# A decoder layer on one core: where the sums of its modulation are kept, who forms the first of them, and in what pieces the first columns of the input projection are worked off

## The chip, the core and the metric

The kernel runs on one NeuronCore of a Trainium2 chip. TensorE (PE) multiplies matrices, VectorE (DVE), ScalarE (ACT) and GpSimd (Pool) work element by element, and SyncE (SP) issues the DMA transfers. Each engine works off its own queue in order; semaphores let one engine wait for another. SBUF is the working memory on the chip, PSUM the memory of eight banks of 128 x 512 floats that TensorE writes its products to. The metric is the time of one execution on the device in microseconds (us), the median of several runs.

## The reference, cut to what matters

One layer for 512 positions and a model width of 2048. A conditioning vector gives a shift, a scale and a gate; the input is normalised, scaled and shifted, and multiplied with one wide matrix whose columns feed two branches.

```python
cond = jax.nn.silu(c)
mod = cond @ w_ada[l] + b_ada[l]                  # 2048 x 6144
shift, scale, gate = jnp.split(mod, 3, axis=-1)
h = rms_norm(x, norm_g[l]) * (1.0 + scale[:, None, :]) + shift[:, None, :]
z = h @ w_in[l]                                   # 2048 x 7184
...
y = jnp.concatenate([y_a, y_b], axis=-1) @ w_out[l]
x = x + gate[:, None, :] * y
```

Everything is in float32. Shift and scale alone need two thirds of `w_ada`, 33.6 MB, before the last part of `h` is known.

## The kernel before, in words

**Products in three.** A float32 product is made of three passes of a faster type: each operand is split into a high and a low half, and TensorE adds high x high, high x low and low x high into one PSUM bank (`mm_cols`, L143 to L145). ACT makes the high half of a weight tile (`whi`, L127), and DVE or Pool subtracts to get the low half (`wlo`, L128). The halves of `h` are `hh` and `hl`.

**The start.** `x` is loaded in four row tiles, each is squared and summed on ACT (`junk`, L311), scaled on DVE (L313) and transposed on TensorE; ACT copies the transposed blocks out as `xT` (L325). Rows of 128 columns of the model width are the 16 k-blocks. For each k-block the shift and the scale are needed, and these are sums over the 2048 rows of `w_ada`. They are not formed on TensorE: a vector engine multiplies each block of 128 rows (`ada`, loaded by `load`, L104) with a number per partition (`sc`) and adds it to an accumulator, sixteen times per group of k-blocks, and a short matmul with a column of ones (`mod`, L267, one pass per k-block and half) then adds over the partitions. `ADA` lists the nine groups: k-blocks 0 and 1 alone, then seven groups of two. `make_h` turns a group's totals into `sh` and `gs` (L272 to L274, DVE), makes `hh` on ACT (L278), a second scaled copy of `xT` on ACT (L286) and `hl` on Pool (L289).

**Where the sums lie, before.** For groups 0 and 1 there are two accumulators of 256 columns in SBUF (`acca`, L237 and L239), used in turns, all on DVE. For groups 2 to 8 the accumulator `acc` lies in PSUM, in the one bank of the tag "c" (L251, L253), and only the last of the sixteen steps writes to SBUF (`accs`). The totals `mod` use the same bank, so a group's sums begin when the totals of the group ahead have been read.

**The first columns.** While `w_ada` streams in, 14 column blocks of 128 (`s`, in two sets of seven) are worked off k-block by k-block, in chunks `CH`: within a chunk first one set over the chunk's k-blocks, then the other. Seven banks hold one set, so at a change of set it is put aside in SBUF (`sp`): ACT copies it the first time (L407), DVE adds it after that (L410). Weights come in tiles of one k-block in the first chunk and of two after that, 512 or 384 columns wide (`raw_st`, then `whi_st` and `wlo_st`, with two buffers each). Pool makes their low halves, but for the two tiles of k-block 0 that come with Pool left out (`q or kk`, L389). Steps of the sums of the next chunk's groups are spread between the weight tiles. After this stage come the attention branch, the gating branch and the output projection, nearly all TensorE; none of that is touched.

**The order.** The scheduler orders each engine's queue ahead of time, from the order of the program and priorities (`high_priority`, `issue_after`). All loads go through SP in one queue. TensorE's queue holds each `mod` at a fixed place between the products.

Of the kernel before, what the change touches and what calls it, by code (L numbers as in the profile page):

```python
# [27 lines left out]
def trunk_kernel(  # L28
# [17 lines left out]
    nc = tc.nc  # L46
# [21 lines left out]

# [1 line left out]
    ident = const.tile([P, P], F32, name="ident")  # L70
# [21 lines left out]

# [1 line left out]
    queue = []  # L94
# [72 lines left out]

# [6 lines left out]
    nc.sync.dma_start(rows[16:32, :], norm_g[0].rearrange("(a b) -> a b", b=P))
    nc.sync.dma_start(rows[32:64, :], b_ada[0, 0 : 2 * D].rearrange("(a b) -> a b", b=P))
    nc.sync.dma_start(rows[64:72, :], ln_g[0].rearrange("(a b) -> a b", b=P))
    nc.sync.dma_start(rows[72:80, :], ln_b[0].rearrange("(a b) -> a b", b=P))

    xt = []
# [23 lines left out]
    WARM = 4
    wbank = bank("c", "warm")

    def warm(src, n):
        for i in range(n):
            nc.tensor.matmul(wbank[:, 0:128], ident, src, start=True, stop=True)

    ADA = [(0, 1), (1, 1), (2, 2), (4, 2), (6, 2), (8, 2), (10, 2), (12, 2), (14, 2)]  # L210
    LANE = "DEDE"

    def ada_step(q, i):
        k0, nk = ADA[q]
        w = nk * P
        per = 4 // nk
        ga = st.tile([P, per, 2, w], F32, name=f"ada{q}_{i}", tag="ada", bufs=8)
        for s in range(2):
            load(
                ga[:, :, s, :], ada_r[:, i * per : (i + 1) * per, s, k0 * P : k0 * P + w]  # L220
            )
        if q == 0:
            warm(ga[:, 0, 1, :], WARM)
        if q in SPL:
            if i == 0:
                three = st.tile([P, 2, 256], F32, name=f"acca{q}", tag="acc", bufs=2)
                accs[q] = {
                    "D": three[:, 0, :].rearrange("p (s n) -> p s n", s=2),
                    "E": three[:, 1, :].rearrange("p (s n) -> p s n", s=2),
                }  # L230
            for j in range(per):
                kk = i * per + j
                ln = LANE[j]
                a = accs[q][ln]
                eng = nc.vector
                if i == 0 and ln not in LANE[:j]:
                    eng.tensor_scalar(a, ga[:, j], sc[:, kk : kk + 1], None, ALU.mult)  # L237
                else:
                    eng.scalar_tensor_tensor(a, ga[:, j], sc[:, kk : kk + 1], a, ALU.mult, ALU.add)  # L239
            return  # L240
        if i == 0:
            accs[q] = (
                bank("c", f"acc{q}"), st.tile([P, 2, 256], F32, name=f"accs{q}", tag="acc", bufs=2)
            )
        pt = accs[q][0]
        a = pt[:, 0 : 2 * w].rearrange("p (s n) -> p s n", s=2)
        sb = accs[q][1][:, :, 0:w]
        for j in range(per):
            kk = i * per + j
            if kk == 0:  # L250
                nc.vector.tensor_scalar(a, ga[:, j], sc[:, kk : kk + 1], None, ALU.mult)  # L251
            else:
                nc.vector.scalar_tensor_tensor(  # L253
                    sb if kk == KB - 1 else a, ga[:, j], sc[:, kk : kk + 1], a,
                    ALU.mult, ALU.add,
                )

    xT = []

    def make_h(q):  # L260
        k0, nk = ADA[q]
        mp = bank("c", f"mod{q}")
        parts = list(accs[q].values()) if q in SPL else [accs[q][1]]
        for s in range(2):
            for j in range(nk):
                for n, part in enumerate(parts):
                    newest_mm[0] = nc.tensor.matmul(  # L267
                        mp[:, s * nk + j : s * nk + j + 1], part[:, s, j * P : (j + 1) * P],
                        ones[:, 0:1], start=(n == 0), stop=(n == len(parts) - 1),
                    )  # L270
        ks = slice(k0, k0 + nk)
        nc.vector.tensor_tensor(sh[:, ks], mp[:, 0:nk], bshT[:, ks], ALU.add)  # L272
        nc.vector.tensor_tensor(gs[:, ks], mp[:, nk : 2 * nk], b1[:, ks], ALU.add)
        nc.vector.tensor_tensor(gs[:, ks], gs[:, ks], ngT[:, ks], ALU.mult)  # L274
        for k in range(k0, k0 + nk):
            hh[k] = act.tile([P, S], F32R, tag="hh", name=f"hh{k}")
            hl[k] = act.tile([P, S], F32R, tag="hl", name=f"hl{k}")
            nc.scalar.activation(  # L278
                hh[k], xT[k], AF.Identity, bias=sh[:, k : k + 1], scale=gs[:, k : k + 1]
            )  # L280
            if q == 0:
                nc.vector.tensor_scalar(
                    xT[k], xT[k], gs[:, k : k + 1], sh[:, k : k + 1], ALU.mult, ALU.add
                )
            else:
                nc.scalar.activation(  # L286
                    xT[k], xT[k], AF.Identity, bias=sh[:, k : k + 1], scale=gs[:, k : k + 1]
                )
            (nc.vector if q == 0 else HL).tensor_tensor(hl[k], xT[k], hh[k].bitcast(F32), ALU.subtract)  # L289
# [19 lines left out]
    for t in range(NT):  # L309
# [3 lines left out]
        XS.tensor_scalar(xt[t], xt[t], rstd[:, t : t + 1], None, ALU.mult)  # L313
    HB = 8
    for kb in range(KB):
        tp = bank("b" if kb % 3 == 2 else "mm", f"xTp{kb}")
        with ExitStack() as es:
            if kb > HB:
                es.enter_context(tc.issue_after(newest_mm[0].ins))
            for t in range(NT):  # L320
                nc.tensor.transpose(
                    tp[:, t * P : (t + 1) * P], xt[t][:, kb * P : (kb + 1) * P], ident
                )
        xk = act.tile([P, S], F32, tag="y", name=f"xT{kb}")
        nc.scalar.activation(xk, tp, AF.Copy)  # L325
# [37 lines left out]
    for q, (k0, nk) in enumerate(CH):  # L363
# [56 lines left out]

# [1 line left out]
    pb_cm = tc.tile_pool(name="pb", bufs=1)  # L422
# [272 lines left out]

# [77 lines left out]

# [110 lines left out]
```

## Time and profile before

| | |
|---|---|
| median of 3 runs | 942.1 us (942.01 to 943.24) |
| span of the profiled execution | 944.6 us |
| PE busy | 902.9 us (96%) |
| DVE / ACT / Pool busy | 555.3 / 413.0 / 127.8 us |
| first and last product of the first columns | 32.4 and 204.2 us |
| bytes read from HBM | 137.54 MB |

The span is counted from the first to the last instruction of the profiled execution; its own time isn't listed apart, and the span is 0.3% over the median of the runs shown. In the profile a row of a timeline names the start, the duration, the engine, the line, the output and the inputs, and in square brackets the idle time ahead of the row and what ended it. A row of a group gives the busy time, the mean of one and the idle time ahead. PEclk is the clock granted to TensorE, with 1.00 as full.

### The profile page before, as it was taken

How to read it: one execution, taken by the hardware profiler on the slowest of the kernel's cores; microseconds unless marked ns; L12 is line 12 of the kernel's file. 1: busy time of each engine (PE TensorE's matmuls, PEld its weight loads, DVE VectorE, ACT ScalarE, POOL GpSimd, SP SyncE). 2: the span in 40 equal slices, each digit the busy share in tenths (PEclk: the TensorE clock that was granted, in tenths of full speed). 3: DMA queues.
4: the chain of work that ended last, by engine and by line, in shares of the span. 5: the costliest groups of instructions: out<-in, count | busy, mean ns of one | idle time of the engine just before them, and what ended most of it. 6: DMA issues, size and time to landing. Idle time of an engine off the chain costs nothing.

```text
span 944.6 us, 12321 instructions
## 1 busy us (share of the span) xinstructions
PE 902.9 (96%) x4485; PEld 764.7 (81%) x4485; DVE 555.3 (59%) x970; ACT 413.0 (44%) x724; POOL 127.8 (14%) x110
## 2 busy tenths in 40 slices
PE   4889989999999999999999999999999998999995
PEld 4768878888888888988899888988888776878884
DVE  4777877473744455546445653757558986555522
ACT  4734423352645545665455644655315322234211
POOL 1136545514000000000000000000002220000000
PEclk9999999999999999999999999999999999999998
DMA  8999996335333232322222333344554555656222
GB/s 297 335 356 351 320 306 185 90 72 146 88 115 90 69 111 68 91 72 86 72 85 70 90 90 90 112 157 123 172 185 134 178 168 178 219 203 213 68 101 89
DMA packets 117916, 142.73 MB, mean 151 GB/s; under 512 B 8400, under 2 KB 89504, under 8 KB 117344
## 3 DMA queue, kind: packets, MB, share of 16 engines
q1 hardware_dynamic: 117856, 141.95, 47.9%
q8 instruction: 35, 0.57, 0.3%
q14 instruction: 25, 0.20, 0.1%
HBM read 137.54 MB, written 4.19 MB: 150 GB/s over the span
## 4 chain that ended last, share of the span: by engine, by line
PE 81%; DMA 5%; DVE 4%; issue 2%; ACT 1%; ACTq 0%; POOLq 0%; POOL 0%; DVEq 0%
PE s L143 5%; PE s L145 5%; PE s L144 5%; DMA gate<-in_w_ada_dram 4%; PE vb L153 3%; PE vb L154 3%; PE vb L152 3%; PE q L143 3%; PE gb L144 3%; PE gb L145 3%; PE q L145 3%; PE va L152 3%; PE va L154 3%; PE gb L143 3%; PE q L144 3%; PE va L153 3%
## 5 line engine op out<-in xcount | busy, mean ns | idle before, releaser
L143 PE MATMUL s<-hh,whi_st 128*128 128x512 f32 x224 | 87.3, 408 | 6.8 <-ACT hh L278 6.7
L144 PE MATMUL s<-hl,whi_st 128*128 128x512 f32 x224 | 87.5, 391 | 1.1 <-POOL hl L289 1.1
L152 PE MATMUL wo<-whi_wo,yh 128*128 128x512 f32 x192 | 77.2, 402 | 4.6 <-DVE r L793 4.6
L145 PE MATMUL s<-hh,wlo_st 128*128 128x512 f32 x224 | 77.4, 391 | 0.0
L603 DVE SCALAR_TENSOR_TENSOR gate<-gate,sc,gate 128x512 f32<-128x512 f32 x60 | 46.9, 782 | 50.6 <-DMA gate<-in_w_ada_dram 50.1
L153 PE MATMUL wo<-whi_wo,yl 128*128 128x512 f32 x192 | 76.2, 397 | 0.0
L253 DVE SCALAR_TENSOR_TENSOR acc<-ada,sc,acc 128x512 f32<-128x512 f32 x98 | 74.0, 755 | 3.1
L128 POOL TENSOR_TENSOR wlo_st<-raw_st,whi_st 128x1024 fp32r<-128x1024 f32 (+3 forms) x32 | 63.8, 1998 | 79.8 <-ACT whi_st L127 78.3
L154 PE MATMUL wo<-wlo_wo,yh 128*128 128x512 f32 x192 | 70.4, 399 | 3.5 <-DVE wlo_wo L128 3.5
L153 PE MATMUL vb<-whi_vb,hl 128*128 128x256 f32 (+1 forms) x256 | 71.7, 286 | 0.0
L152 PE MATMUL vb<-whi_vb,hh 128*128 128x256 f32 (+1 forms) x256 | 71.3, 284 | 0.0
L154 PE MATMUL vb<-wlo_vb,hh 128*128 128x256 f32 (+1 forms) x256 | 67.5, 285 | 0.0
L127 ACT ACTIVATE whi_st<-raw_st 128x1024 fp32r<-128x1024 f32 (+3 forms) x36 | 31.4, 873 | 78.7 <-PE s L144 29.3
L143 PEld LDWEIGHTS s<-hh,whi_st 128*128 128x128 f32 x224 | 43.4, 195 | 16.5 <-ACT hh L278 7.0
L143 PE MATMUL q<-hh,whi_q 128*128 128x512 f32 x128 | 50.5, 395 | 1.6 <-ACT ft L662 1.6
L144 PEld LDWEIGHTS s<-hl,whi_st 128*128 128x128 f32 x224 | 42.2, 188 | 10.9 <-POOL hl L289 2.3
L144 PE MATMUL gb<-hl,whi_gb 128*128 128x512 f32 x128 | 50.4, 394 | 0.0
L152 PE MATMUL va<-whi_va,hh 128*128 128x512 f32 x128 | 50.4, 395 | 0.0
L143 PE MATMUL gb<-hh,whi_gb 128*128 128x512 f32 x128 | 50.1, 391 | 0.0
L144 PE MATMUL q<-hl,whi_q 128*128 128x512 f32 x128 | 50.0, 391 | 0.0
L145 PE MATMUL gb<-hh,wlo_gb 128*128 128x512 f32 x128 | 50.0, 393 | 0.0
L153 PE MATMUL va<-whi_va,hl 128*128 128x512 f32 x128 | 50.0, 390 | 0.0
(220 smaller groups left out, 2204.5 us busy)
## 6 DMA issues: line engine op xcount, KB each, us to landing
ada<-in_w_ada_dram SPq DMA_DIRECT2D x128, 256.0 KB
gate<-in_w_ada_dram SPq DMA_DIRECT2D x32, 512.0 KB
raw_wo<-in_w_out_dram SPq DMA_DIRECT2D x24, 512.0 KB
raw_q<-in_w_in_dram SPq DMA_DIRECT2D x16, 512.0 KB
raw_k<-in_w_in_dram SPq DMA_DIRECT2D x16, 512.0 KB
raw_gb<-in_w_in_dram SPq DMA_DIRECT2D x16, 512.0 KB
raw_va<-in_w_in_dram SPq DMA_DIRECT2D x16, 512.0 KB
raw_st<-in_w_in_dram SPq DMA_DIRECT2D x21, 384.0 KB
```

Source lines behind the costliest of these rows:

```text
L127: nc.scalar.activation(hi, raw, AF.Copy)
L128: (loeng or nc.vector).tensor_tensor(lo, raw, hi.bitcast(F32), ALU.subtract)
L143: nc.tensor.matmul(pt, hi[:, j, cs], hh[k], start=(k == first), stop=False)
L144: nc.tensor.matmul(pt, hi[:, j, cs], hl[k], start=False, stop=False)
L145: nc.tensor.matmul(pt, lo[:, j, cs], hh[k], start=False, stop=(k == last))
L152: nc.tensor.matmul(o, ah[k][:, tsl], hi[:, j, :], start=(k == first), stop=False)
L153: nc.tensor.matmul(o, al[k][:, tsl], hi[:, j, :], start=False, stop=False)
L154: nc.tensor.matmul(o, ah[k][:, tsl], lo[:, j, :], start=False, stop=(k == last))
L253: nc.vector.scalar_tensor_tensor(sb if kk == KB - 1 else a, ga[:, j], sc[:, kk : kk + 1], a, ALU.mult, ALU.add,)
L603: nc.vector.scalar_tensor_tensor(a, ga[:, j], sc[:, kk : kk + 1], a, ALU.mult, ALU.add)
```

## The change

**Sums.** The accumulators of groups 2 to 8 move from PSUM to SBUF (`accs`, two buffers), for all sixteen steps; the bank of tag "c" holds the totals only (and, at the start, the columns and the target of the warming products). Group 0's steps are shared: of each four rows, DVE takes three and ACT multiplies the fourth, which Pool adds to a second accumulator (lanes "DADD"). Group 1 keeps two lanes on DVE and may not begin ahead of the last sum of group 0.

**Chunks.** `CH` becomes (0,1), (1,1), (2,2), (4,2), (6,2), (8,4), (12,4): k-blocks 0 and 1 are chunks of their own, with tiles of one k-block, and the last four blocks one chunk. The low halves of all tiles of `s` go to Pool.

**Start.** The small vectors are loaded through ACT's queue, `c` in a tile of its own, so that `x` stands first on SP. The products that only keep TensorE busy are other ones: 18 at once and 7 after each row tile, in bfloat16, 384 columns wide, in place of 16 over `ada` tiles. `make_h` is given a higher priority; copies of `xT` beyond block 6 come behind the first `hh`.

```diff
-            accs[q] = (
-                bank("c", f"acc{q}"), st.tile([P, 2, 256], F32, name=f"accs{q}", tag="acc", bufs=2)
-            )
-        pt = accs[q][0]
-        a = pt[:, 0 : 2 * w].rearrange("p (s n) -> p s n", s=2)
-        sb = accs[q][1][:, :, 0:w]
+            accs[q] = st.tile([P, 2, 256], F32, name=f"accs{q}", tag="acc", bufs=2)
+        a = accs[q][:, :, 0:w]
...
                 nc.vector.scalar_tensor_tensor(
-                    sb if kk == KB - 1 else a, ga[:, j], sc[:, kk : kk + 1], a,
-                    ALU.mult, ALU.add,
+                    a, ga[:, j], sc[:, kk : kk + 1], a, ALU.mult, ALU.add
                 )
...
-    LANE = "DEDE"
+    LANES = {0: "DADD", 1: "DEDE"}
...
+                if ln == "A":
+                    dst = a if begin else ga[:, j]
+                    nc.scalar.activation(dst, ga[:, j], AF.Copy, scale=sc[:, kk : kk + 1])
+                    if not begin:
+                        nc.gpsimd.tensor_tensor(a, a, dst, ALU.add)
...
+    def warm(src, n):
+        for _ in range(n):
+            nc.tensor.matmul(wbank[:, P:S], cmask[:, 0:P], src, start=True, stop=True)
+
+    warm(cmask[:, P:S], BUSY)
...
-    nc.sync.dma_start(rows[0:16, :], c[0].rearrange("(a b) -> a b", b=P))
+    crow = st.tile([16, P], F32, name="crow")
+    nc.scalar.dma_start(crow, c[0].rearrange("(a b) -> a b", b=P))
...
-    CH = [(0, 2), (2, 2), (4, 2), (6, 2), (8, 4), (12, 2), (14, 2)]
+    CH = [(0, 1), (1, 1), (2, 2), (4, 2), (6, 2), (8, 4), (12, 4)]
...
-        st_k = 1 if q == 0 else 2
+        st_k = min(nk, 2)
...
-                        loeng=nc.gpsimd if gi in POOLG and (q or kk) else None,
+                        loeng=nc.gpsimd if gi in POOLG else None,
```

What the scheduler makes of it is seen in three places. In the rows a digit after a name is the group or the chunk, the number behind it a buffer.

DVE before, at the end of group 2's sums and the beginning of group 3's:

```order
L253 SCALAR_TENSOR_TENSOR acc2_420<-ada2_7_517,sc_110,acc2_420 128x512
L253 SCALAR_TENSOR_TENSOR accs2_421<-ada2_7_517,sc_110,acc2_420 128x512
L272 TENSOR_TENSOR sh_118<-mod2_522,cols_108 128x2
L273 TENSOR_TENSOR gs_117<-mod2_522,b1_115 128x2
L274 TENSOR_TENSOR gs_117<-gs_117,cols_108 128x2
L251 TENSOR_SCALAR acc3_608<-ada3_0_605,sc_110 128x512
L253 SCALAR_TENSOR_TENSOR acc3_608<-ada3_0_605,sc_110,acc3_608 128x512
```

The same place with the change (L264 and L266 are the sums now, L285 to L287 the totals' use):

```order
L266 SCALAR_TENSOR_TENSOR accs2_504<-ada2_7_584,sc_131,accs2_504 128x512 x2
L264 TENSOR_SCALAR accs3_655<-ada3_0_652,sc_131 128x512
L266 SCALAR_TENSOR_TENSOR accs3_655<-ada3_0_652,sc_131,accs3_655 128x512
L266 SCALAR_TENSOR_TENSOR accs3_655<-ada3_1_658,sc_131,accs3_655 128x512 x2
L285 TENSOR_TENSOR sh_139<-mod2_589,cols_126 128x2
L286 TENSOR_TENSOR gs_138<-mod2_589,b1_136 128x2
L266 SCALAR_TENSOR_TENSOR accs3_655<-ada3_2_663,sc_131,accs3_655 128x512
L287 TENSOR_TENSOR gs_138<-gs_138,cols_126 128x2
```

Four sums of the next group now stand ahead of the use of a group's totals, where before the totals came first; and both inputs of a sum, `ada` and `accs`, lie in SBUF.

TensorE before, where k-block 10 begins (`mod6` holds the totals of k-blocks 10 and 11):

```order
L145 MATMUL s3_6_1090<-hh9_1050,wlo_st4_0_1_8_1228 128x512
L267 MATMUL mod6_1141<-ones_85,accs6_1059 128x1 x4
L143 MATMUL s3_0_1084<-hh10_1149,whi_st4_0_0_10_1261 128x512
L143 MATMUL s3_1_1085<-hh10_1149,whi_st4_0_0_10_1261 128x512
L143 MATMUL s3_2_1086<-hh10_1149,whi_st4_0_0_10_1261 128x512
```

TensorE with the change, around the same totals and where k-block 10 begins:

```order
L146 MATMUL s4_10_1130<-hl8_1090,whi_st5_1_0_8_1230 128x512
L280 MATMUL mod6_1185<-ones_85,accs6_1102 128x1 x4
L147 MATMUL s4_7_1127<-hh8_1089,wlo_st5_1_0_8_1231 128x512
...
L147 MATMUL s4_13_1133<-hh9_1094,wlo_st5_1_1_8_1277 128x512
L145 MATMUL s4_7_1127<-hh10_1193,whi_st5_1_0_10_1316 128x512
```

The totals stood right ahead of the first product that needs them; they now stand 34 products ahead of it. The same holds for the group of k-blocks 2 and 3 (none between before, 14 now).

Pool with the change, from the first row tiles to k-block 1 (`acca0` is the shared lane of group 0):

```order
L245 TENSOR_TENSOR acca0_144<-acca0_144,ada0_1_149 128x256
L245 TENSOR_TENSOR acca0_144<-acca0_144,ada0_2_157 128x256
L245 TENSOR_TENSOR acca0_144<-acca0_144,ada0_3_165 128x256
L130 TENSOR_TENSOR wlo_st0_0_0_0_362<-raw_st0_0_0_0_359,whi_st0_0_0_0_361 128x512
L130 TENSOR_TENSOR wlo_st0_0_1_0_395<-raw_st0_0_1_0_392,whi_st0_0_1_0_394 128x384
L130 TENSOR_TENSOR wlo_st0_1_0_0_452<-raw_st0_1_0_0_448,whi_st0_1_0_0_451 128x512
L303 TENSOR_TENSOR hl1_430<-xT1_235,hh1_429 128x512
```

Before, Pool's first work in this place was the tile of k-block 1; the three additions and the tiles of k-block 0 are new there. Behind the last product of the first columns TensorE's queue is the same, row for row, before and with the change.

More of the change, by code (lines that the diff above doesn't have):

```diff
@@ L57, in trunk_kernel @@
     turn = [0]
+    BUSY = 18
+    WARM = 7
     def bank(tag, name):
@@ L170, in trunk_kernel @@
     st = st_cm.__enter__()
-    rows = st.tile([80, P], F32, name="rows")
-    nc.sync.dma_start(rows[0:16, :], c[0].rearrange("(a b) -> a b", b=P))
[L174 to L177, printed above, removed]
+    crow = st.tile([16, P], F32, name="crow")
+    nc.scalar.dma_start(crow, c[0].rearrange("(a b) -> a b", b=P))
+    rows = st.tile([64, P], F32, name="rows")
+    for r0, nr, src in (
+        (16, 32, b_ada[0, 0 : 2 * D]), (0, 16, norm_g[0]), (48, 8, ln_g[0]), (56, 8, ln_b[0]),
+    ):
+        nc.scalar.dma_start(rows[r0 : r0 + nr, :], src.rearrange("(a b) -> a b", b=P))
     xt = []
@@ L183, in trunk_kernel @@
         xt.append(xx)
-    cols_p = bank("c", "cols_p")
-    nc.tensor.transpose(cols_p[:, 0:80], rows, ident[0:80, 0:80])
+    wbank = bank("c", "warm")
+    def warm(src, n):
+        for _ in range(n):
+            nc.tensor.matmul(wbank[:, P:S], cmask[:, 0:P], src, start=True, stop=True)
+    warm(cmask[:, P:S], BUSY)
+    cols_p = wbank
     cols = const.tile([P, 80], F32, name="cols")
-    nc.vector.tensor_copy(cols, cols_p[:, 0:80])
+    nc.tensor.transpose(cols_p[:, 0:16], crow, ident[0:16, 0:16])
+    nc.vector.tensor_copy(cols[:, 0:16], cols_p[:, 0:16])
+    nc.tensor.transpose(cols_p[:, 16:80], rows, ident[0:64, 0:64])
+    nc.vector.tensor_copy(cols[:, 16:80], cols_p[:, 16:80])
     cT, ngT, bshT, bscT, lngb = (cols[:, 16 * i : 16 * (i + 1)] for i in range(5))
@@ L200, in trunk_kernel @@
     accs = {}
+    end0 = [None]
     gate = gp_.tile([P, 4, 512], F32, name="gate")
     SPL = (0, 1)
[L203 to L208, printed above, removed]
     ADA = [(0, 1), (1, 1), (2, 2), (4, 2), (6, 2), (8, 2), (10, 2), (12, 2), (14, 2)]
-    LANE = "DEDE"
+    LANES = {0: "DADD", 1: "DEDE"}
     def ada_step(q, i):
@@ L221, in ada_step @@
             )
-        if q == 0:
-            warm(ga[:, 0, 1, :], WARM)
         if q in SPL:
@@ L227, in ada_step @@
                 accs[q] = {
-                    "D": three[:, 0, :].rearrange("p (s n) -> p s n", s=2),
-                    "E": three[:, 1, :].rearrange("p (s n) -> p s n", s=2),
+                    ln: three[:, z, :].rearrange("p (s n) -> p s n", s=2)
+                    for z, ln in enumerate(sorted(set(LANES[q])))
                 }
@@ L232, in ada_step @@
                 kk = i * per + j
-                ln = LANE[j]
+                ln = LANES[q][j]
                 a = accs[q][ln]
-                eng = nc.vector
-                if i == 0 and ln not in LANE[:j]:
-                    eng.tensor_scalar(a, ga[:, j], sc[:, kk : kk + 1], None, ALU.mult)
-                else:
-                    eng.scalar_tensor_tensor(a, ga[:, j], sc[:, kk : kk + 1], a, ALU.mult, ALU.add)
+                begin = i == 0 and ln not in LANES[q][:j]
+                if ln == "A":
[3 more added lines that the diff above has]
+                        nc.gpsimd.tensor_tensor(a, a, dst, ALU.add)
+                elif begin:
+                    with ExitStack() as es:
+                        if q:
+                            es.enter_context(tc.issue_after(end0[0].ins))
+                        nc.vector.tensor_scalar(a, ga[:, j], sc[:, kk : kk + 1], None, ALU.mult)
+                else:
+                    z = nc.vector.scalar_tensor_tensor(
+                        a, ga[:, j], sc[:, kk : kk + 1], a, ALU.mult, ALU.add
+                    )
+                    if q == 0:
+                        end0[0] = z
             return
         if i == 0:
-            accs[q] = (
-                bank("c", f"acc{q}"), st.tile([P, 2, 256], F32, name=f"accs{q}", tag="acc", bufs=2)
-            )
-        pt = accs[q][0]
-        a = pt[:, 0 : 2 * w].rearrange("p (s n) -> p s n", s=2)
-        sb = accs[q][1][:, :, 0:w]
+            accs[q] = st.tile([P, 2, 256], F32, name=f"accs{q}", tag="acc", bufs=2)
+        a = accs[q][:, :, 0:w]
         for j in range(per):
@@ L253, in ada_step @@
                 nc.vector.scalar_tensor_tensor(
-                    sb if kk == KB - 1 else a, ga[:, j], sc[:, kk : kk + 1], a,
-                    ALU.mult, ALU.add,
+                    a, ga[:, j], sc[:, kk : kk + 1], a, ALU.mult, ALU.add
                 )
     xT = []
+    first_h = [None]
     def make_h(q):
@@ L262, in make_h @@
         mp = bank("c", f"mod{q}")
-        parts = list(accs[q].values()) if q in SPL else [accs[q][1]]
+        parts = list(accs[q].values()) if q in SPL else [accs[q]]
         for s in range(2):
@@ L277, in make_h @@
             hl[k] = act.tile([P, S], F32R, tag="hl", name=f"hl{k}")
-            nc.scalar.activation(
+            z = nc.scalar.activation(
                 hh[k], xT[k], AF.Identity, bias=sh[:, k : k + 1], scale=gs[:, k : k + 1]
@@ L281, in make_h @@
             if q == 0:
+                first_h[0] = z
                 nc.vector.tensor_scalar(
@@ L296, in end @@
             ada_step(q, n - 1)
-            make_h(q)
+            with tc.high_priority(offset=200):
+                make_h(q)
         return st_ + [end]
-    CH = [(0, 2), (2, 2), (4, 2), (6, 2), (8, 4), (12, 2), (14, 2)]
-    for i in range(4):
-        ada_step(0, i)
+    CH = [(0, 1), (1, 1), (2, 2), (4, 2), (6, 2), (8, 4), (12, 4)]
+    with tc.high_priority(offset=200):
+        for i in range(4):
+            ada_step(0, i)
     XS = nc.vector
@@ L313, in trunk_kernel @@
         XS.tensor_scalar(xt[t], xt[t], rstd[:, t : t + 1], None, ALU.mult)
-    HB = 8
+        warm(junk[:, P:S], WARM)
+    HB = 6
     for kb in range(KB):
-        tp = bank("b" if kb % 3 == 2 else "mm", f"xTp{kb}")
+        tp = bank("b" if kb in (4, 5, 6) or kb > 10 else "mm", f"xTp{kb}")
+        for t in range(NT):
+            nc.tensor.transpose(
+                tp[:, t * P : (t + 1) * P], xt[t][:, kb * P : (kb + 1) * P], ident
+            )
+        xk = act.tile([P, S], F32, tag="y", name=f"xT{kb}")
         with ExitStack() as es:
             if kb > HB:
[L319 to L325, printed above, removed]
+                es.enter_context(tc.issue_after(first_h[0].ins))
+            nc.scalar.activation(xk, tp, AF.Copy)
         xT.append(xk)
```

## The prediction

> **What bounds the kernel now.** I read the page first, then busy time by stretches, then TensorE's timeline at its waits, then the groups of DVE and Pool, and at last the places where those two work at the same time. The stretches are the start, the first columns, all the rest, one pair of k-blocks in the middle of the first columns, and the surroundings of two waits; the columns are the length, the busy time of each engine, the granted clock, the DMA share and GB/s.
>
> ```profile
> span 944.6 us, 12321 instructions
> ...
> core 0: us, PE busy (x) PEld busy (x) DVE busy (x) ACT busy (x) POOL busy (x), PEclk, DMA share, GB/s
> 0.00:32.40 32.40, 17.99 (x104) 16.48 (x105) 19.86 (x51) 18.02 (x27) 4.18 (x14) 0.95 0.96 300
> 32.40:204.30 171.90, 164.01 (x739) 134.96 (x738) 121.00 (x187) 68.64 (x94) 82.61 (x47) 0.98 0.82 257
> 204.30:944.60 740.30, 720.95 (x3646) 613.27 (x3644) 414.41 (x734) 326.31 (x604) 40.99 (x49) 0.99 0.38 120
> 92.20:112.40 20.20, 20.20 (x96) 16.83 (x95) 16.57 (x26) 6.76 (x8) 11.20 (x7) 1.00 1.03 339
> 58.00:62.00 4.00, 3.12 (x7) 1.97 (x7) 3.82 (x6) 2.36 (x4) 4.00 (x3) 0.57 1.09 356
> 132.00:138.00 6.00, 3.91 (x11) 3.12 (x12) 5.79 (x8) 2.93 (x4) 3.65 (x3) 0.72 0.92 279
> ```
>
> TensorE is busy for 164.0 of the 171.9 us of the first columns, so it sets their end. The 740 us behind them keep their order on TensorE and are left as they are: what the change does is what it does to the moment 204.3. In one pair of k-blocks TensorE is full, DVE works 16.6 of 20.2 us and Pool 11.2: neither is a bound as long as they work side by side. TensorE's waits in this stage, and the totals of two neighbouring groups:
>
> ```profile
> 58.30 3.12 PE L143 MATMUL s<-hh,whi_st 128*128 128x512 f32 x7 [2.51 <-ACT hh L278]
> 72.28 0.95 PE L267 MATMUL mod<-ones,accs 128*128 128x1 f32 x8
> 92.26 0.95 PE L267 MATMUL mod<-ones,accs 128*128 128x1 f32 x8
> 134.09 2.50 PE L143 MATMUL s<-hh,whi_st 128*128 128x512 f32 x5 [2.71 <-ACT hh L278]
> ```
>
> Between the totals at 72.28 and 92.26 lie 84 products and one set of totals, so a product takes (19.98 - 0.95) / 84 = 0.2265 us. The long waits also cost clock: 0.57 granted over 4 us at 58 is 1.7 us lost, 0.72 over 6 us at 132 about 1.5 (the fall to 0.92 while it waited costs nothing).
>
> **The change part by part.**
>
> *The start and the places of the totals.* Five small loads go from SP to ACT's queue. SP's first load of `x` and the weight that TensorE and ACT wait for at k-block 2:
>
> ```profile
> 2.89 2.07 SPq L104 DMA_DIRECT2D x<-in_x_dram  x4
> 33.71 0.48 DVE L239 SCALAR_TENSOR_TENSOR acca<-ada,sc,acca 128x256 f32<-128x256 f32 x1
> 55.64 1.90 ACT L127 ACTIVATE whi_st<-raw_st 128x1024 fp32r<-128x1024 f32 x2 [5.52 <-DMA raw_st<-in_w_in_dram]
> ```
>
> SP began its issues at 0.80, so the stream of loads can begin 2.1 us earlier. On ACT the five issues cost about as much, and end ahead of the first `x`. The weight at 55.64 came behind 17.0 MB by my count of the loads ahead of it; in the new order the last tile of k-block 1 comes behind the same 17.0 MB, so at about 53.5. TensorE waits there for it as it waited at 58.30, and from there I take it 2.3 us ahead of before (bounds 0 and 3.4). The sums of group 0 on three engines, the priority of `make_h` and the warming products bring the first product forward, but that ends in the same wait for data: 0. Of what is new there, Pool's three additions of 256 columns lie between half of a 512-column subtraction (0.65 each) and that whole with a sum ahead of it (2.0), 2 to 6 us spread over 6 us of arriving data, and end at most some 4 us late, under the same wait. The warming products are bfloat16 and no row shows one; with 0.2265 us for 512 columns as an upper end at full clock and twice that at half, 28 of them take 0 to 13 us between the row tiles, and up to 3 us of delay there is covered by the wait at 53.5. The wait at 134.09 goes, with the totals 34 products (7.7 us) ahead: from the totals at 130.43 to the product at 134.09 it took 3.7. That is 2.7 + 1.5 = 4.2 us. The larger last chunk moves no work off TensorE: 0. By these parts alone the first columns end 6.5 us earlier.
>
> *The sums in SBUF.* This is the part that decides. Groups of DVE and Pool over the whole run, the range of one sum in PSUM (least, median, most, in ns), and two neighbouring spill additions:
>
> ```profile
> L253 DVE SCALAR_TENSOR_TENSOR acc<-ada,sc,acc 128x512 f32<-128x512 f32 x98 | 74.0, 755 | 3.1
> L603 DVE SCALAR_TENSOR_TENSOR gate<-gate,sc,gate 128x512 f32<-128x512 f32 x60 | 46.9, 782 | 50.6 <-DMA gate<-in_w_ada_dram 50.1
> ...
> L128 POOL TENSOR_TENSOR wlo_st<-raw_st,whi_st 128x1024 fp32r<-128x1024 f32 x14 | 33.6, 2398 | 41.6 <-ACT whi_st L127 41.6
> L128 POOL TENSOR_TENSOR wlo_st<-raw_st,whi_st 128x768 fp32r<-128x768 f32 x14 | 25.8, 1841 | 12.5 <-ACT whi_st L127 11.0 <-DVE sp L410 1.5
> L289 POOL TENSOR_TENSOR hl<-xT,hh 128x512 fp32r<-128x512 f32 x15 | 19.1, 1294 | 16.3 <-ACT xT L286 16.3
> ...
> L253 DVE SCALAR_TENSOR_TENSOR acc<-ada,sc,acc x98: 745/756/757, 39.6 to 169.2; 128x512 f32<-128x512 f32 x98
> ...
> 86.36 1.28 DVE L410 TENSOR_TENSOR sp<-s,sp 128x512 f32<-128x512 f32 x2
> 93.24 0.16 DVE L272 TENSOR_TENSOR sh<-mod,cols 128x2 f32<-128x2 f32 x1 [1.84 <-PE mod L267]
> ```
>
> With one input in PSUM all 98 sums took 745 to 757 ns, though Pool was at work for half of that time. The gate's sums are the same instruction with both inputs in SBUF, as the change makes all of them, and they show what happens when Pool works on SBUF beside them:
>
> ```profile
> 750.25 1.79 DVE L603 SCALAR_TENSOR_TENSOR gate<-gate,sc,gate 128x512 f32<-128x512 f32 x1 [1.26 <-DMA gate<-in_w_ada_dram]
> 751.96 1.77 DVE L67 TENSOR_TENSOR yl<-y,yh 128x512 fp32r<-128x512 f32 x1
> 753.65 0.47 DVE L748 SCALAR_TENSOR_TENSOR mt<-mix,cols,mt 128x256 f32<-128x256 f32 x1
> 755.89 1.77 DVE L603 SCALAR_TENSOR_TENSOR gate<-gate,sc,gate 128x512 f32<-128x512 f32 x1
> ...
> 750.20 1.29 POOL L67 TENSOR_TENSOR yl<-y,yh 128x512 fp32r<-128x512 f32 x1 [19.88 <-ACT yh L66]
> 751.45 7.37 POOL L67 TENSOR_TENSOR vl<-va,vh 128x512 fp32r<-128x512 f32 x4
> ```
>
> A sum of 0.75 us takes 1.79 beside one Pool subtraction of 512 columns, and each of the four subtractions takes 1.84 where the first took 1.29; the `mt` row, with `mix` in PSUM, isn't held up: 0.47 for 256 columns. The two take turns. A Pool instruction of 512 columns thus costs DVE 1.79 - 0.75 = 1.04 us, or 1.77 - 0.75 = 1.02, and 1.09 for the other kind: I take 1.05.
>
> Now the queue of DVE from the start of group 2's sums to the end of group 8's. Start: group 1's last sum stood at 33.7; 2.1 earlier, and 2 later for what Pool holds up: 33.5. Seven groups of sixteen sums: 112 x 0.755 = 84.6 us. Spill additions: 28 x 0.64 = 17.9. Totals: 7 x 3 x 0.16 = 3.3. Together 105.8, which ends at 139. TensorE, without any hold-up, would come to the last totals at 204.3 - 6.5 - 46.8 = 151 (behind them stand 202 products, 202 x 0.2265 = 45.8, and the totals' 0.95). So DVE has 12 us to spare, and it must now wait for Pool. In units of 512 columns Pool does by then: ten pairs of large tiles, 10 x 3.5; the small tiles of k-blocks 0 and 1 that are left, 5.25; 12 of the `hl`. That is 52 units, 54.6 us at 1.05. If all of it falls on the sums, the last totals are ready at 33.5 + 105.8 + 54.6 = 193.9; if as much as can lies under DVE's other work, at 33.5 + 84.6 + 54.6 = 172.7; shared out by DVE's time (84.6 / 105.8 = 0.80 of it on sums), at 183.0. I take the last, since the spill additions stand mixed among the sums in the new order. Then 0.95 + 45.8, and 1.7 for a clock that has fallen while TensorE waited: the first columns end at 231.4 (221 to 242), 27 us after 204.3 (17 to 38). The earlier start and the lost wait are hidden by this: TensorE waits for totals anyway.
>
> [...]
>
> The profiled execution's span of 944.6 lies 2.5 us over the median of 942.1; I put the difference on the median: 942.1 + 27 = 969.
>
> **The rivals.**
>
> *The sums don't collide here (faster).* If a unit costs DVE under 12 / 54.6 of 1.05, some 0.23 us, the totals stay ahead of TensorE and the 6.5 us are won: 935.6; up to 0.35 us it is still no slower than before. For it: the 98 sums of before ran beside Pool undisturbed, and Pool idles 9 us in a pair of k-blocks, in which sums may fall. Against it: the rows at 750 to 757, same instruction, same operands. 15%.
>
> *The collision is milder.* Pool's instructions find DVE at the spill additions or without data more than I think; half the blocked time is 22 us, the totals come at 161, and the end moves by 5: 943 to 957. 10%.
>
> *Pool starves.* These rows show Pool's tiny instruction behind DVE, and the same without DVE:
>
> ```profile
> 720.96 1.28 DVE L67 TENSOR_TENSOR vl<-va,vh 128x512 fp32r<-128x512 f32 x2
> 722.16 1.28 DVE L67 TENSOR_TENSOR yl<-y,yh 128x512 fp32r<-128x512 f32 x2
> ...
> 721.12 2.73 POOL L91 TENSOR_TENSOR rsv<-rsv,nhalf 128x1 f32<-128x1 f32 x1 [5.25 <-DVE rsv L90]
> 9.96 0.55 POOL L91 TENSOR_TENSOR rstd<-rstd,nhalf 128x1 f32<-128x1 f32 x1 [7.52 <-DVE rstd L90]
> ```
>
> It took 2.73 for 0.55: it sat through four instructions of DVE. If runs of sums hold Pool off in that way, low halves come late as well; 2.2 us at one tile of each of the seven groups, beside the 27 to 38, gives 980 to 995. 12%.
>
> *No change to be seen.* A measurement of this kernel tells about 0.2%, 1.9 us, from nothing. Gain and loss would have to cancel: 942. 3%.
>
> **How the numbers follow.** The forecast, DVE's queue late by 17 to 38 us (959 to 980), has 60%; its middle is 969. Slower is 60 + 10 + 12 = 82%, the same 3%, faster 15%. The range leaves out the fast rival (15%) and the upper end of the starved one: 947 to 985.
>
> **What would show it.** In the profile after, the sums `accs` should have a mean of 1.1 to 1.3 us where 0.755 stood, with single ones near 1.8 and, beside the large tiles, near 3; Pool's large tiles should go over 2.4 us; TensorE should wait several us for `accs` at the totals of groups 5 to 8; the last product of the first columns should start near 231; and the wait at `hh` of k-block 10 should be gone. I am wrong if the sums stay near 0.76, or if they are long and TensorE still doesn't wait at the totals.

## The result, and the profile after

The changed kernel takes **964.8 us** (962.3 to 967.6, 4 runs), the kernel before beside it 942.2: a ratio of 1.023, 95% interval 1.0202 to 1.0259. It is slower by 22.6 us. The profiled execution of the changed kernel took 967.6 us, with a span of 965.9.

I read the same views as of before, and first the stretches: the start, the first columns, all the rest, and what lies behind the last totals.

```profile
0.00:32.40 32.40, 23.29 (x116) 15.82 (x116) 19.75 (x45) 18.60 (x29) 9.17 (x19) 0.81 0.96 295
32.40:231.60 199.20, 173.76 (x742) 137.77 (x742) 159.09 (x186) 68.67 (x96) 98.22 (x49) 0.95 0.71 223
231.60:965.90 734.30, 718.80 (x3646) 612.15 (x3644) 414.29 (x734) 325.97 (x604) 40.67 (x49) 0.99 0.39 121
185.00:231.60 46.60, 46.58 (x210) 38.74 (x211) 11.19 (x20) 18.92 (x25) 19.47 (x10) 1.00 0.28 72
```

Counted from 32.4 us in both kernels, the first columns last 199.2 us where they lasted 171.9. TensorE stands idle in them for 199.2 - 173.8 = 25.4 us, 17.5 more than the 7.9 of before. Its busy time grew by another 9.8, of which the lower granted clock makes some 5 (164.0 x 0.98 / 0.95 = 169.2); the rest isn't explained. Behind the last totals, 46.6 us, it is full.

DVE is what changed most. From 33.5 us, about the end of group 1's sums, to the last totals, with the change and then before:

```profile
33.50:185.00 151.50, 126.09 (x529) 98.13 (x528) 146.79 (x164) 48.66 (x69) 78.75 (x39) 0.94 0.84 269
33.50:178.00 144.50, 136.61 (x617) 112.27 (x616) 108.89 (x167) 52.45 (x71) 71.61 (x41) 0.98 0.91 290
```

DVE works 146.8 of 151.5 us, where it worked 108.9 of 144.5: its queue has next to no gaps now, and TensorE has them. The groups of DVE and Pool (busy time, mean of one):

```profile
L266 DVE SCALAR_TENSOR_TENSOR accs<-ada,sc,accs 128x512 f32<-128x512 f32 x105 | 127.1, 1212 | 3.1 <-DMA ada<-in_w_ada_dram 0.5
L427 DVE TENSOR_TENSOR sp<-s,sp 128x512 f32<-128x512 f32 x42 | 28.2, 683 | 34.3 <-PE s L147 34.3
...
L130 POOL TENSOR_TENSOR wlo_st<-raw_st,whi_st 128x1024 fp32r<-128x1024 f32 x14 | 36.5, 2609 | 28.6 <-ACT whi_st L129 18.5 <-issue 5.6 <-PE s L147 4.6
L130 POOL TENSOR_TENSOR wlo_st<-raw_st,whi_st 128x768 fp32r<-128x768 f32 x14 | 29.1, 2082 | 23.5 <-ACT whi_st L129 23.5
L303 POOL TENSOR_TENSOR hl<-xT,hh 128x512 fp32r<-128x512 f32 x15 | 23.6, 1595 | 37.5 <-ACT xT L300 37.5
```

The least, the median and the longest of the sums:

```profile
L266 DVE SCALAR_TENSOR_TENSOR accs<-ada,sc,accs x105: 734/752/2774, 36.3 to 184.1; 128x512 f32<-128x512 f32 x105
```

Who held TensorE up between 32 and 232 (us in all, times, longest):

```profile
PE mod L280 <- DVE accs L266: 11.3, 5, 2.7
PE s L147 <- POOL wlo_st L130: 8.1, 7, 2.0
PE s L145 <- ACT whi_st L129: 5.4, 3, 2.8
PE s L145 <- DVE sp L427: 0.7, 1, 0.7
```

The sums rose from 0.755 to a mean of 1.212 us, but their median stayed at 752 ns: more than half ran undisturbed, and the loss sits in the others, up to 2.77 us. The spill additions, which read PSUM, took 0.683 on the mean, 0.686 before, and weren't held up: the nine that ran beside an instruction of Pool took 0.673 to 0.685. Pool's large tiles went from 2.40 to 2.61. TensorE's idle time is 11.3 us at totals, and 13.5 at low and high halves that came late. One wait of each kind, the wait at the last totals, and the last product of the first columns:

```profile
60.09 0.51 PE L145 MATMUL s<-hh,whi_st 128*128 128x512 f32 x1 [2.77 <-ACT whi_st L129]
144.08 1.02 PE L280 MATMUL mod<-ones,accs 128*128 128x1 f32 x8 [2.69 <-DVE accs L266]
156.79 0.69 PE L147 MATMUL s<-hh,wlo_st 128*128 128x512 f32 x1 [2.04 <-POOL wlo_st L130]
185.03 1.02 PE L280 MATMUL mod<-ones,accs 128*128 128x1 f32 x8 [2.56 <-DVE accs L266]
231.58 0.39 PE L147 MATMUL s<-hh,wlo_st 128*128 128x512 f32 x1
```

Two places show one collision each. Of DVE's timeline the sum:

```profile
71.52 2.56 DVE L266 SCALAR_TENSOR_TENSOR accs<-ada,sc,accs 128x512 f32<-128x512 f32 x1
123.33 2.27 DVE L266 SCALAR_TENSOR_TENSOR accs<-ada,sc,accs 128x512 f32<-128x512 f32 x1
```

Of Pool's the tile:

```profile
71.13 2.40 POOL L130 TENSOR_TENSOR wlo_st<-raw_st,whi_st 128x1024 fp32r<-128x1024 f32 x1 [2.72 <-ACT whi_st L129]
122.22 2.82 POOL L130 TENSOR_TENSOR wlo_st<-raw_st,whi_st 128x1024 fp32r<-128x1024 f32 x1 [5.61 <-issue]
```

At 71.13 Pool's tile starts first and runs its usual 2.40 us, to 73.53; the sum that starts beside it ends at 74.08, 0.55 later. At 122.22 the tile ends at 125.04 and the sum at 125.60. In both some 0.55 of the 0.75 us that a sum takes alone lie behind the tile's end: the sum waited for nearly all that was left of the tile. The trace has this throughout. From the first to the last of these sums Pool has 39 instructions and DVE 39 sums of over 1 us; each of these sums stands beside another one of the 39, and ends 0.54 to 0.56 us after it.

### The profile page after: what moved, and what is told of

It is laid out like the page before. It is cut to its first block, busy times and chain, and to the rows that moved or that the text cites. A ratio compares the mean times of both kernels' runs of the same rounds, so it can differ in the third digit from the quotient of the medians.

```text
span 965.9 us, 12367 instructions
## 1 busy us (share of the span) xinstructions
PE 915.8 (95%) x4500; PEld 765.7 (79%) x4500; DVE 593.1 (61%) x963; ACT 413.2 (43%) x728; POOL 148.1 (15%) x117
## 4 chain that ended last, share of the span: by engine, by line
PE 70%; DVE 16%; DMA 7%; issue 4%; ACT 1%; SPq 0%; POOL 0%; ACTq 0%; POOLq 0%; DVEq 0%
DVE accs L266 11%; DMA gate<-in_w_ada_dram 4%; PE vb L155 3%; PE vb L156 3%; PE vb L154 3%; PE q L145 3%; PE gb L146 3%; PE gb L147 3%; PE q L147 3%; PE gb L145 3%; PE q L146 3%; PE k L145 3%; PE k L147 3%; PE k L146 3%; PE wo L156 3%
## 5 line engine op out<-in xcount | busy, mean ns | idle before, releaser
L266 DVE SCALAR_TENSOR_TENSOR accs<-ada,sc,accs 128x512 f32<-128x512 f32 x105 | 127.1, 1212 | 3.1 <-DMA ada<-in_w_ada_dram 0.5
L145 PE MATMUL s<-hh,whi_st 128*128 128x512 f32 x224 | 90.8, 413 | 8.4 <-ACT whi_st L129 5.4
L146 PE MATMUL s<-hl,whi_st 128*128 128x512 f32 x224 | 89.7, 405 | 0.0
L130 POOL TENSOR_TENSOR wlo_st<-raw_st,whi_st 128x1024 fp32r<-128x1024 f32 (+3 forms) x36 | 77.5, 2162 | 64.6 <-ACT whi_st L129 47.3
L620 DVE SCALAR_TENSOR_TENSOR gate<-gate,sc,gate 128x512 f32<-128x512 f32 x60 | 46.6, 777 | 47.5 <-DMA gate<-in_w_ada_dram 47.1
L129 ACT ACTIVATE whi_st<-raw_st 128x1024 fp32r<-128x1024 f32 (+3 forms) x36 | 31.0, 866 | 73.1 <-PE s L146 43.7
L147 PEld LDWEIGHTS s<-hh,wlo_st 128*128 128x128 f32 x224 | 44.1, 197 | 20.9 <-POOL wlo_st L130 11.7
```

The source lines that it names most:

```text
L129: nc.scalar.activation(hi, raw, AF.Copy)
L130: (loeng or nc.vector).tensor_tensor(lo, raw, hi.bitcast(F32), ALU.subtract)
L145: nc.tensor.matmul(pt, hi[:, j, cs], hh[k], start=(k == first), stop=False)
L146: nc.tensor.matmul(pt, hi[:, j, cs], hl[k], start=False, stop=False)
L147: nc.tensor.matmul(pt, lo[:, j, cs], hh[k], start=False, stop=(k == last))
L266: nc.vector.scalar_tensor_tensor(a, ga[:, j], sc[:, kk : kk + 1], a, ALU.mult, ALU.add)
```

## The experiments

All ratios are to the kernel before, run on the same chip beside each. The letters in the expectations: A is the prediction's theory (DVE's sums and Pool's subtractions, both on SBUF, take turns, and DVE's longer queue sets the end); B, that the loss lies in other parts of the change; C, that a sum with both inputs in SBUF is slow by itself. D and F are explained where they come.

### The change with its sums back in PSUM

```
-            accs[q] = st.tile([P, 2, 256], F32, name=f"accs{q}", tag="acc", bufs=2)
+            accs[q] = (bank("c", f"acc{q}"), st.tile([P, 2, 256], F32, ...))
```

and the lines of before that use it.

> The changed kernel with one part undone: the sums of groups 2 to 8 lie in PSUM again, the rest stays. Theory A (a sum with both inputs in SBUF and a Pool instruction take turns): the mean of a sum falls from 1.21 to 0.755 us and Pool's large tiles from 2.6 to 2.4; no wait of TensorE names a late sum. But with the one bank shared again the scheduler puts the totals right ahead of their first product at k-blocks 2, 4, 6, 8 and 10, and each such place cost 4.2 us before (2.7 and the clock): four more of them on 936 gives some 948 to 956. Theory B (the chunks, the tiles of one k-block and the new order cost the time, wherever the sums lie): it stays at 965 within 4.

Measured: 949.4 us (946.0 to 951.9, 8 runs), 1.0052 (1.0029 to 1.0074). Its sums have the 755 ns of before, and TensorE doesn't wait for `accs` at totals:

```profile
L270 DVE SCALAR_TENSOR_TENSOR acc<-ada,sc,acc 128x512 f32<-128x512 f32 x98 | 74.0, 755 | 3.1
```

The waits that are left, for `hh` and `hl`:

```profile
PE s L145 <- ACT hh L296: 7.2, 5, 2.7
PE s L146 <- POOL hl L308: 2.7, 3, 1.6
```

Some 17 us of the 22 are the sums' (1.0230 to 1.0052), and B falls. The rest has another cause: in its order the totals of k-blocks 2 to 11 stand 0 to 3 products ahead of the first product that needs them, so that TensorE waits at `hh` five times.

### The kernel before with its sums in SBUF, and nothing else

The reverse edit on the kernel before.

> The kernel before with one part of the change alone: the sums of groups 2 to 8 in SBUF. Theory A: the mean of a sum goes from 0.755 to 1.2 us, TensorE waits for late totals, and the time is 962 to 972, all of the loss or a little more, since the start is the old one. Theory B: 942 within 2, the sums at 0.76.

Measured: 963.7 us (963.3 to 964.7, 4 runs), 1.0202 (1.0172 to 1.0232). Its sums:

```profile
L249 DVE SCALAR_TENSOR_TENSOR accs<-ada,sc,accs 128x512 f32<-128x512 f32 x105 | 114.8, 1096 | 2.4
```

Its two longest waits at totals:

```profile
71.05 0.56 PE L262 MATMUL mod<-ones,accs 128*128 128x1 f32 x2 [5.47 <-DVE accs L249]
94.59 1.03 PE L262 MATMUL mod<-ones,accs 128*128 128x1 f32 x8 [2.76 <-DVE accs L249]
```

The first step of a group has only one input in SBUF, and its output (least, median, longest):

```profile
L247 DVE TENSOR_SCALAR accs<-ada,sc x7: 473/481/2616, 34.5 to 157.9; 128x512 f32<-128x512 f32 x7
```

Two of these seven took 2.0 and 2.6 us for 0.48, and both ended 0.28 us after a tile of Pool that they met. So two inputs in SBUF are not the only form that Pool holds up.

The one edit alone gives nearly the whole loss. A holds.

### The change with all low halves on DVE

```
-    HL = nc.gpsimd
+    HL = nc.vector
...
-                        loeng=nc.gpsimd if gi in POOLG else None,
+                        loeng=None,
```

> The changed kernel with the low halves of the weights and of h made by DVE in place of Pool, the sums in SBUF as they are. Theory A: with Pool idle nothing takes turns, the sums fall to 0.755, and DVE's queue to the last totals is 33.5 + 105.8 + 52 x 0.61 = 171 in place of 185 us: 948 to 955, faster than with Pool's help. Theory C (a sum to SBUF is slow by itself, for its output or its chain): the sums stay near 1.2 and DVE's queue grows by 32 us: 990 or more. Theory B: 965 or more, since DVE has more to do.

Measured: 946.8 us (944.3 to 949.9, 10 runs), 1.0030 (1.0009 to 1.0052), a little below what was expected. The sums and the large tiles, both on DVE now:

```profile
L266 DVE SCALAR_TENSOR_TENSOR accs<-ada,sc,accs 128x512 f32<-128x512 f32 x105 | 75.7, 745 | 1.0
L130 DVE TENSOR_TENSOR wlo_st<-raw_st,whi_st 128x1024 fp32r<-128x1024 f32 x14 | 17.1, 1218 | 10.2 <-ACT whi_st L129 10.1
```

The longest of TensorE's waits that are left:

```profile
102.26 2.93 PE L145 MATMUL s<-hh,whi_st 128*128 128x512 f32 x7 [3.26 <-ACT hh L291]
```

C falls: with Pool silent the same sums on SBUF take 745 ns. With the sums in SBUF, Pool's help is worse than none (1.0230 against 1.0030): a large tile takes DVE 1.22 us and Pool 2.40 undisturbed, 1.97 times as long, and what was left of Pool's instruction was lost to DVE at each of the 39 sums that it held up.

### The change with only the wide tiles on Pool

```
-    HL = nc.gpsimd
-    POOLG = (0, 1)
+    HL = nc.vector
+    POOLG = (0,)
```

> The changed kernel with Pool left the low halves of the wider tile of each pair only; the narrower ones and those of h go to DVE. Theory A, by the sum: 23 of the 52 units stay on Pool and cost DVE 0.8 x 1.05 each, 29 cost it 0.61 each, so the last totals come some 7 us ahead of the changed kernel's and 7 behind the one without Pool: 953 to 960, the mean of a sum near 0.95. If instead one Pool instruction in the way costs as much as many: 962 or more.

Measured: 960.3 us (959.2 to 960.7, 4 runs), 1.0174 (1.0149 to 1.0198): a little over the upper end, though the sums are shorter than expected:

```profile
L266 DVE SCALAR_TENSOR_TENSOR accs<-ada,sc,accs 128x512 f32<-128x512 f32 x105 | 89.0, 863 | 1.5
```

TensorE's two longest waits:

```profile
109.99 3.24 PE L145 MATMUL s<-hh,whi_st 128*128 128x512 f32 x7 [3.44 <-ACT hh L291]
149.56 3.35 PE L145 MATMUL s<-hh,whi_st 128*128 128x512 f32 x7 [7.12 <-ACT hh L291]
```

The sums lost (863 - 745) x 105 = 12 us, not 49, but DVE took over the narrow tiles, and the order came out otherwise: the totals of k-blocks 6 and 10 now stand 3 and 0 products ahead of their first use (55 and 34 in the changed kernel), and there TensorE waits 10.6 us. As a half dose the run is inconclusive, since the place of the totals moved with it.

### The kernel before with the new chunks only

```
-    CH = [(0, 2), (2, 2), (4, 2), (6, 2), (8, 4), (12, 2), (14, 2)]
+    CH = [(0, 1), (1, 1), (2, 2), (4, 2), (6, 2), (8, 4), (12, 4)]
...
-        st_k = 1 if q == 0 else 2
+        st_k = min(nk, 2)
```

> The kernel before with another part alone: the chunks of 1, 1, 2, 2, 2, 4, 4 k-blocks, the sums in PSUM. Theory A: the sums stay at 0.755; what it costs comes from the totals that now stand right ahead of their first product at k-blocks 2, 4, 6, 8 and 10 in place of 2 and 10: three more places of 4.2 us, 948 to 957. Theory B: 960 to 968, nearly all of the loss.

Measured: 951.8 us (949.9 to 956.2, 6 runs), 1.0081 (1.0054 to 1.0109), as expected. TensorE's waits at `hh` and `hl`:

```profile
PE s L143 <- ACT hh L278: 9.5, 5, 2.7
PE s L144 <- POOL hl L289: 3.4, 4, 0.9
```

With the sums in PSUM the new chunks cost some 8 us by themselves: as in the first experiment, the totals come 0 to 3 products ahead of the product that needs them, five times.

### Chunks of two throughout, with the new start and without it

Both kernels have their sums in PSUM, `CH` as eight chunks of two k-blocks and `st_k` as before. The first is the first experiment with that, the second the kernel before.

> The start of the changed kernel, the sums of groups 2 to 8 in PSUM, and chunks of two k-blocks throughout (0,2), (2,2) ... (14,2), by which the totals of all groups from k-block 4 on stand 34 products ahead of the first that needs them. Theory A puts the loss on the shared reads of DVE and Pool alone and holds the early start and the lost wait for a gain of 6.5 us: 934 to 939, sums at 0.755, one wait of some 3 us at k-block 2 left. A rival, that the start gains nothing since TensorE waits for data at k-block 2 anyway: 938 to 941.

> The kernel before with chunks of two k-blocks throughout and nothing else: the totals of k-block 10 move from right ahead of their first product to 34 products ahead. By the price of that wait (2.7 us and 1.5 of clock) 938 to 940 against 942 to 943; one more change of set adds seven spill additions, 4.8 us on DVE, which has room. The rival: the wait is hidden by data that would be late anyway, 942 to 944.

Measured: 937.5 us (934.2 to 939.7, 6 runs), 0.9929 (0.9904 to 0.9954), and 937.4 us (936.1 to 941.1, 6 runs), 0.9939 (0.9916 to 0.9962). The waits at `hh`, first with the new start, then without:

```profile
58.66 1.43 PE L145 MATMUL s<-hh,whi_st 128*128 128x512 f32 x4 [2.06 <-ACT hh L296]
```

```profile
58.14 2.47 PE L143 MATMUL s<-hh,whi_st 128*128 128x512 f32 x7 [2.18 <-ACT hh L278]
```

Both beat both kernels of this case. The wait at k-block 10 is gone, as every group's totals from k-block 4 on now stand 34 products ahead; that is worth 5.8 us (3.6 to 7.9). The new start adds nothing that these runs can tell: TensorE waits at the same place, at 58, in both.

The kernel with the new start also shows that an output in SBUF is not what collides. The last sum of each group reads its accumulator in PSUM and writes to SBUF (least, median, longest):

```profile
L270 DVE SCALAR_TENSOR_TENSOR accs<-ada,sc,acc x7: 748/748/750, 50.8 to 170.4; 128x512 f32<-128x512 f32 x7
```

Five of the seven ran beside an instruction of Pool, and none was held up.

### Chunks of two with the sums in SBUF

The changed kernel whole, with the chunks of the two kernels above. D is the theory that the loss needs the change's own chunks.

> The changed kernel whole, its sums in SBUF, but with the first columns in eight chunks of two k-blocks. The same with its sums in PSUM measured 937.5 us, with the sums at a mean of 0.755 us. In this order the totals stand 24 to 118 products ahead of the first product that needs them, so late totals have more slack than in any kernel here. Theory A (sums with both inputs in SBUF take turns with Pool, whatever the chunks, and DVE's queue then is the bound, so slack at the totals does not help): 950 to 958, mean of the sums 1.1 to 1.25 us, TensorE again waits for `accs` at totals. Rival D (the loss needs the changed kernel's chunks, where totals or low halves are wanted at a bad moment): under 945, though the sums may be as long.

Measured: 963.2 us (962.8 to 966.1, 5 runs), 1.0211 (1.0181 to 1.0242). D falls, and A's figure was too low by 5 us. The sums:

```profile
L266 DVE SCALAR_TENSOR_TENSOR accs<-ada,sc,accs 128x512 f32<-128x512 f32 x105 | 122.4, 1169 | 2.4
```

The longest and the last wait at totals:

```profile
116.71 1.84 PE L280 MATMUL mod<-ones,accs 128*128 128x1 f32 x8 [4.21 <-DVE accs L266]
163.00 1.39 PE L280 MATMUL mod<-ones,accs 128*128 128x1 f32 x8 [1.58 <-DVE accs L266]
```

Totals that stand 24 to 118 products ahead of their use, from k-block 2 on, don't help. Three kernels with other chunks and starts, side by side:

| chunks and start | sums in PSUM | sums in SBUF |
|---|---|---|
| those of before | 1 | 1.0202 |
| those of the change | 1.0052 | 1.0230 |
| chunks of two, start of the change | 0.9929 | 1.0211 |

With the sums in PSUM the three lie 1.2% apart; with the sums in SBUF 0.3%. That fits a bound that does not lie on TensorE (in the kernel of this section DVE works 144.5 of the 151.5 us from 33.5 to 185): what is gained or lost on TensorE then no longer counts.

### The change without the low halves of its weight tiles

```
-                        loeng=nc.gpsimd if gi in POOLG else None,
+                        nolo=True,
```

where `nolo` makes `w_tile` return the high half twice. F is the theory that the new chunks cost time of their own here too.

> The changed kernel with the low halves of the weight tiles of the first columns left out (TensorE multiplies by the high half a second time in their place, so that its number of products is the same; the output is not the reference's). The order of the totals is almost that of the changed kernel. Only `hl` is left of Pool's work beside the sums, 15 instructions. Theory A (the collision is the loss): sums at a mean of 0.82 to 0.9 us, no wait for `accs` at the totals, last product of the first columns at 198 to 206, 934 to 943 us, which would also show the 6.5 us that the prediction gave to a kernel without collisions. Rival F (the new chunks and the order of the totals cost something of their own, as they do with the sums in PSUM): 946 to 952 with the sums as short as that. This kernel cannot tell DVE's lost time from low halves that come late, since both go.

Measured: 934.2 us (931.9 to 936.3, 6 runs), 0.9895 (0.9865 to 0.9926). Its first columns and what follows:

```profile
32.40:197.90 165.50, 161.65 (x735) 133.95 (x736) 123.40 (x184) 68.36 (x93) 22.34 (x15) 0.99 0.83 264
197.90:931.10 733.20, 718.50 (x3646) 612.45 (x3645) 414.25 (x734) 325.65 (x604) 40.53 (x49) 0.99 0.39 121
```

Its sums:

```profile
L268 DVE SCALAR_TENSOR_TENSOR accs<-ada,sc,accs 128x512 f32<-128x512 f32 x105 | 91.2, 869 | 5.6 <-DMA ada<-in_w_ada_dram 2.7
```

The only waits of over 1 us for weights in that stage:

```profile
53.00 0.50 PE L147 MATMUL s<-hh,whi_st 128*128 128x512 f32 x1 [1.51 <-ACT whi_st L128]
57.41 1.43 PE L147 MATMUL s<-hh,whi_st 128*128 128x512 f32 x4 [2.08 <-ACT whi_st L128]
```

With `hl` alone left to meet, the sums fall to 0.87 us, TensorE doesn't wait at totals there, and the first columns end at 198. F falls: with nearly the order of the change, no time is lost. Everything that is lost by the change is gone with Pool's subtractions of the weight tiles; how much of it was DVE's queue and how much low halves that came late, this kernel can't tell.

## Why the prediction came out as it did

The forecast was 969 us (947 to 985); 964.8 was measured. The mechanism was the one named, and it was at work where it was put.

**The collision's price.** The prediction put 52 units of 512 columns beside DVE, 54.6 us, and 43.7 of it on sums. Pool's groups in the changed kernel between 33.5 and 185 us:

```profile
L130 POOL TENSOR_TENSOR wlo_st<-raw_st,whi_st 128x1024 fp32r<-128x1024 f32 x10 | 26.9, 2695 | 17.2 <-ACT whi_st L129 7.1 <-issue 5.6 <-PE s L147 4.6
L130 POOL TENSOR_TENSOR wlo_st<-raw_st,whi_st 128x768 fp32r<-128x768 f32 x10 | 21.8, 2176 | 18.1 <-ACT whi_st L129 18.1
L303 POOL TENSOR_TENSOR hl<-xT,hh 128x512 fp32r<-128x512 f32 x13 | 21.1, 1641 | 31.5 <-ACT xT L300 31.5
L130 POOL TENSOR_TENSOR wlo_st<-raw_st,whi_st 128x512 fp32r<-128x512 f32 x3 | 5.1, 1696 | 7.2 <-DMA ada<-in_w_ada_dram 7.1
L130 POOL TENSOR_TENSOR wlo_st<-raw_st,whi_st 128x384 fp32r<-128x384 f32 x3 | 4.5, 1500 | 0.6 <-ACT whi_st L129 0.6
```

These are 20 + 15 + 13 + 3 + 2.25 = 53 units, and the sums lost 105 x (1.212 - 0.745) = 49.0 us, with 0.745 from the run with Pool silent. The term was 5 us too small: 0.92 us a unit, where 1.05 and a share of 0.80 make 0.84.

Both factors were off, in opposite directions. The share was 1: each of these 39 instructions of Pool held up a sum, and of the 79 us that they took only some 4 lay beside DVE's other work. And the price of a unit isn't fixed. A sum that began while Pool was at work lost what was left of Pool's instruction, less some 0.2 us (0.55 to 0.75); over the 39 that came to 49.0 / 39 = 1.26 us, or 0.92 a unit and not 1.05. The trace shows it at each of them: 39 of 39 sums ended 0.54 to 0.56 us behind Pool's instruction. Such a sum paid only for the rest of the instruction (on the mean 1.45 of its 2.04 us).

**The queue's end.** Last totals at 185.0 (forecast 183.0), last product of the first columns at 231.6 (231.4). That these are so near is in part luck. Group 2's sums began at 35.8 and not at 33.5; the collisions cost 49.0 and not 43.7; the rest of the queue took 184.9 - 35.8 - 49.0 = 100.1 us and not 105.8. The three come to 2 us. Behind the totals the 1.7 us for a fallen clock weren't paid (granted 1.00 from 185 on), and that makes up for the 2. That the earlier start and the lost wait would be hidden is borne out by the table above.

**What TensorE waits for.** "TensorE should wait several us for `accs` at the totals of groups 5 to 8" failed in its size and in part in its places: there were five such waits of 1.6 to 2.7 us, 11.3 in all, at groups 2, 4, 5, 6 and 8. Another 13.5 us went to late high and low halves. Two of the three waits for high halves, 4.7 of their 5.4 us (at 60.1 and 82.8), come from DVE's queue too. ACT made the tile behind `hh`, and for `hh` it had stood idle until DVE's `gs`:

```profile
56.69 1.52 ACT L291 ACTIVATE hh<-xT,sh,gs 128x512 fp32r<-128x512 f32 x2 [5.07 <-DVE gs L287]
80.47 1.52 ACT L291 ACTIVATE hh<-xT,sh,gs 128x512 fp32r<-128x512 f32 x2 [9.42 <-DVE gs L287]
```

How much of the waits for low halves goes back to the same queue isn't settled. A part of the Pool rival was thus there, seven waits for low halves with 8.1 us, but with the waits at the totals shorter in turn, and not on top of the 27 us; the 980 to 995 it gave fell.

**The start.** Data were to be late at about 53.5. In the run without low halves TensorE waits at 53.0 for a tile whose data were late (ACT stood idle 3.80 us for them), and at 57.4 for one that ACT made behind other work; in the changed kernel the wait of 2.8 us at 60.1 is the one behind DVE's `gs`. Whether the start gains 2.3 us isn't settled: with and without it, chunks of two give 0.9929 and 0.9939, with intervals of 0.0025 to either side.

**The wait at k-block 10.** It is gone, and chunks of two, where it goes too, gain 5.8 us (3.6 to 7.9) for the 4.2 of the prediction. With Pool's subtractions of weights left out the change came to 934.2, where the prediction gave 935.6 to a change without collisions.

**What stayed as it was.** That "the 740 us behind them" are "left as they are" holds for the order, but their length was the term with the largest error. A second profile of the kernel before (943.3 us) was expected to take 734 to 737 us there if the first was chance, and 740 if not. It has:

```profile
32.40:206.50 174.10, 166.31 (x747) 136.63 (x746) 122.88 (x188) 69.58 (x96) 82.58 (x47) 0.98 0.81 254
206.50:941.60 735.10, 717.26 (x3645) 610.94 (x3643) 413.93 (x734) 326.19 (x604) 40.66 (x49) 1.00 0.39 121
```

The rest took 735.1 us there and 734.3 after: the 740 belonged to that one execution, with the same instructions. Why it was longer isn't shown: the granted clock was 0.99 in it, 1.00 in the second profile and 0.99 after. Against the second profile the first columns grew by 25 us and not by 27. The sum of 231.4 and 740 is thus 6 us too long; the 2.5 taken from the span for the median should have been 1.1 (965.9 to 964.8). That is the 4 us between forecast and result.

The other rivals: the sums do collide (1.212 us), the collision isn't mild (49 of 54.6 us), and no cancelling took place.

## What to carry to other kernels

Before an accumulator moves from PSUM to SBUF, look at what Pool does in the same stretch: in the changed kernel each of the 39 instructions on SBUF that Pool ran among the sums held up one of them, with both its inputs in SBUF, and that sum ended 0.54 to 0.56 us behind it. That cost 0.92 us for each 512 columns that Pool worked on, and 0.59 to 1.00 in the four other kernels with such sums beside Pool, by how many of Pool's instructions met a sum (8 of 12 at the low end, 13 of 13 at the high one). It may then be cheaper to take the work from Pool altogether. When the queue of a side engine sets the end, gains on the main engine can vanish, as they did here (three kernels 1.2% apart with the sums in PSUM, 0.3% with them in SBUF): test each part of a change with the other parts undone. Take a long stage that nothing touches from two profiles, not from one.

## What was unexpected

- With the sums in SBUF, taking all low halves away from Pool and giving them to DVE, which already set the end, gains 2% (1.0230 to 1.0030).
- The new chunks, worth nothing in the prediction's sum, cost 0.8% (0.5 to 1.1) on the kernel before. It is the place that the scheduler gives to the totals which costs: at 0 to 3 products ahead of their use each group made TensorE wait 0.6 to 2.7 us for `hh`, at 34 products ahead not at all.
- The collision stretches few instructions much and not all a little: a median of 752 ns with a mean of 1212.
